# Attention's queue order: transposes ahead of near scores, output copies with the sum of the same step

## The chip, the cores and the metric

The kernel runs on one core of a Trainium2 chip. A core has engines that work side by side, each through its own queue in order: TensorE (matrix products and transposes, PE in the profile), VectorE (DVE), ScalarE (ACT), GpSimd (POOL) and SyncE (SP, which here only issues DMAs). The engines meet through semaphores. TensorE writes to PSUM, a small memory of eight banks; VectorE and ScalarE read results there. The metric is device time in microseconds for one execution.

## The reference

One decoder layer on 2048 tokens of width 1024, in float32: a mixer (attention beside pooling), a gated MLP, a gated embedding and a last norm. The change touches the attention alone: 8 heads of width 64, three dilated sliding windows, mixed by their softmax denominators.

```python
DIL_PATTERNS = ((128, 1), (512, 4), (2048, 16))

def _dilated_branch(q, k, v, slopes, window, dil):
    ...
    s = s - slopes[:, None, None] * dist
    s = jnp.where(valid[:, None, None], s, -jnp.inf)
    m = jnp.max(s, axis=-1, keepdims=True)
    e = jnp.exp(s - m)
    den = jnp.sum(e, axis=-1)
    o = jnp.einsum('bnrhqk,bnkrhd->bnqrhd', e, vv.astype(jnp.float32))
    ...

def _dilated_attention(q, k, v, slopes):
    ...
    w = d * jnp.exp(m - jnp.max(m, axis=0, keepdims=True))
    w = w / jnp.sum(w, axis=0, keepdims=True)
    return jnp.sum(w[..., None] * o, axis=0)
```

## The kernel before

The kernel runs in phases: projection, attention (399 to about 691 us of the profiled span), output product, MLP, gated embedding. Products are done on pairs of float32r tiles, a high part and a low part, to keep float32's precision.

Attention works through 128 steps, 16 blocks of 128 queries for each of 8 heads. In a step the "near" part is the window of stride 1 (up to 256 keys), the "far" part joins the two dilated windows (128 to 512 keys). Inside a group of four steps the blocks are taken in the order 3, 1, 2, 0, so the far part of steps 0, 1, 2 and 3 of a group has 512, 256, 384 and 128 keys. Two heads form a pair; even heads keep their output on partitions 0 to 63, odd heads on 64 to 127.

The order of every engine's queue is written out by hand. The loop at L744 goes through the steps, and for each step through `CFG["ord"]`, a list of pairs of a stage's name and a lag: stage X with lag d works in step s on the block of step s - d. The place in the list sets the order of the instructions in each engine's queue. The stages:

- N, F (`near_scores`, L574 and L575; `far_scores`, L563 and L564): two products each on TensorE, queries' high and low parts. The near scores of all steps share one PSUM bank, even steps in one half, odd steps in the other; far scores have two banks.
- nm, fm (`near_max`, L579; `far_max`, L585), VectorE: bias added, and the extreme of each row. The profile shows them as a custom operation with a short read of the accumulator behind it.
- ne, fe (`near_exp`, L591; `far_exp`, L595), ScalarE: exponentials with their row sums. A stage A allocates their tile.
- T (`turn`, L605), TensorE: 2 to 6 transposes of 128 x 128 into PSUM; two buffers alternate from step to step (tags t and u).
- h (`high`, L618), ScalarE, and l (`low`, L622), VectorE: high and low part of the transposed tile. The low part is the last reader of the transposes' bank.
- V and W (`values`, `values_b`, L633 and L647), TensorE: products with the values. They work on whole groups of four steps: parts 0 and 1 the far output, parts 2 and 3 the near output, into one PSUM tile each.
- o (`fold`, copy at L664), ScalarE: after parts 1 and 3, so in every other step, a copy of the other 64 partitions of the output. It puts the sum that belongs to it into the list `due`. p (`folded`, sum at L665), VectorE: takes everything that lies in `due` and adds.
- S, M (`stats`, `mix`): at the end of a head pair the maxima and denominators are transposed, copied and stored to DRAM, loaded again in another layout (ScalarE's DMAs), turned into weights (small operations on VectorE) and used by GpSimd to mix the outputs.
- B begins a step and issues nothing.

So before, step s holds in each queue, with the lag in brackets: TensorE V(7), W(7), N(0), T(2), F(0); VectorE fm(1), p, l(3), statistics, nm(0); ScalarE M's DMAs, o(7), ne(1), fe(1), h(2).

Of the kernel before, what the change touches and what calls it, by code (L numbers as in the profile page):

```python
# [10 lines left out]
F32 = mybir.dt.float32  # L11
# [6 lines left out]
P = 128  # L18
D = 1024
KD = D // P  # L20
S = 2048
# [5 lines left out]
CH = 512  # L27
# [13 lines left out]
V_N = V_CB + 2 * NF  # L41


CFG = {"tt": 2, "ee": 2, 'ord': [['B', 0], ['A', 1], ['M', 0], ['V', 7], ['fm', 1], ['W', 7], ['N', 0], ['p', 8], ['T', 2], ['F', 0], ['o', 7], ['ne', 1], ['fe', 1], ['h', 2], ['l', 3], ['S', 2], ['nm', 0]], 'perm': [3, 1, 2, 0], 'fp': [[0], [1], [2], [3]], 'np': [[0, -1], [1], [2], [3]], 'm': [9, 10, 13, 4, 6, 7]}


class Shared:
# [438 lines left out]
def phase_attention(tc, g, mx, near_b, far_b):  # L486
# [5 lines left out]
    with ExitStack() as ctx:  # L492
# [4 lines left out]
        ps_o = ctx.enter_context(tc.tile_pool(name="b_o", bufs=2, space=PSUM, reuse_waits="tile"))  # L497
# [37 lines left out]
        def begin(s):  # L535
# [7 lines left out]
            st = steps[s] = Shared()  # L543
            st.n = n = n - n % 4 + CFG["perm"][n % 4]
            st.t, st.pt, st.e = heads[h], pairs[h // 2], h % 2
# [5 lines left out]
            st.d1, st.d3 = st.pt.st1[:, 1, st.e, n : n + 1], st.pt.st3[:, st.r, 1, st.e, st.i : st.i + 1]  # L551
            st.tt = sb.tile([P, 768], F32, tag="tt", bufs=CFG["tt"], name="tt")

        def exp_tile(s):
            steps[s].ee = sb.tile([P, 768], F32, tag="ee", bufs=CFG["ee"], name="ee")

# [67 lines left out]
        def near_pv(gi, kbs, first):  # L624
            gr, q0 = groups[gi], 4 * (gi % 4)
            for kb in kbs:
                if q0 + kb < 0:
                    continue
                m0, m1 = max(0, kb), min(3, kb + 1)
                b0, b1 = 4 * m0 + kb + 1, 4 * m1 + kb + 1  # L630
                kt = q0 + kb
                for pt in (gr.h, gr.l):
                    nc.tensor.matmul(  # L633
                        gr.o[:, m0 * P : (m1 + 1) * P],
                        vals[gi // 8, "v1", kt // 4][:, kt % 4, gi // 4 % 2, :],
                        pt[:, b0 : b1 + 1 : 4, :],
                        start=first,
                        stop=False,
                        skip_group_check=True,
                    )  # L640
                    first = False

        def far_pv(gi, kbs, first):
            gr = groups[gi]
            for kb in kbs:
                for pt in (gr.h, gr.l):
                    nc.tensor.matmul(  # L647
                        gr.o[:, kb * P :],
                        vals[gi // 8, "v3", gi % 4][:, kb, gi // 4 % 2, :],
                        pt[:, 6 * kb + 2 : 18 + kb : 5, :],  # L650
                        start=first,
                        stop=False,
                        skip_group_check=True,
                    )
                    first = False
# [3 lines left out]
        def halves_sum(dst, o, e):  # L659

            mine = slice(DH * e, DH * e + DH)
            other = slice(DH * (1 - e), DH * (1 - e) + DH)
            ev = sb.tile([P, CH], F32, tag="ev", bufs=2, name="ev")
            nc.scalar.copy(ev[mine], o[other])  # L664
            due.append(lambda: nc.vector.tensor_tensor(dst, o[mine], ev[mine], op=ALU.add))  # L665

        def values(v):
            gi, part = v // 4, v % 4
            gr = groups[gi]
            if part % 2 == 0:  # L670
                gr.o = ps_o.tile([P, CH], F32, tag="o", name="o")
            if part < 2:
                far_pv(gi, CFG["fp"][2 * part], part == 0)
            else:
                near_pv(gi, CFG["np"][2 * part - 4], part == 2)

        def values_b(v):
            gi, part = v // 4, v % 4
            if part < 2:
                far_pv(gi, CFG["fp"][2 * part + 1], False)  # L680
            else:
                near_pv(gi, CFG["np"][2 * part - 3], False)

        def fold(v):
            gi, part = v // 4, v % 4
            if part % 2 == 0:
                return
            gr = groups[gi]
            h, q = divmod(gi, 4)
            pt, e = pairs[h // 2], h % 2  # L690
            mine = slice(DH * e, DH * e + DH)
            if part == 1:
                halves_sum(pt.s3[mine, q, :], gr.o, e)
            else:
                halves_sum(pt.s1[mine, q * CH : (q + 1) * CH], gr.o, e)
                groups.pop(gi)

        def folded(v):
# [34 lines left out]
        with tc.manual_schedule(engines=set(EN.values())):  # L733
            for dst, src in load_qk(0):
                rdma(nc, dst, src)
            for q in range(4):
                for which in ("v3", "v1"):
                    rdma(nc, *load_v(0, which, q))
            queue = []
            stages = {  # L740
                "F": far_scores, "N": near_scores, "fm": far_max, "nm": near_max, "fe": far_exp, "ne": near_exp,
                "T": turn, "h": high, "l": low, "V": values, "W": values_b, "S": stats, "M": mix, "o": fold, "p": folded, "B": begin, "A": exp_tile
            }
            for s in range(NS + 10):  # L744
                if s < NS:
                    h, n = divmod(s, NQ)
                    if n == 1 and h + 1 < H:
                        queue += load_qk(h + 1)
                    if queue:
                        rdma(nc, *queue.pop(0))  # L750
                    for pr in range(1, NPAIR):
                        if s - 2 * NQ * (pr - 1) in V_STEPS:
                            rdma(nc, *load_v(pr, *V_STEPS[s - 2 * NQ * (pr - 1)]))
                if s == NS + 2:
                    last_far(nc, g, mx, ps_t, pairs[NPAIR - 1])
                    pieces = pairs[NPAIR - 1].pieces = last_weights(nc, mx, pairs[NPAIR - 1])
                for nm, lag in CFG["ord"]:
                    if 0 <= s - lag < NS or nm == "M":
                        stages[nm](s - lag)
                for _ in range({NS + 3: 3, NS + 4: 2, NS + 5: 1}.get(s, 0)):  # L760
                    next(pieces)
# [1214 lines left out]
```

## Time and profile before

| | us |
|---|---|
| median of 3 runs | 2417.68 (2416.0 to 2421.61) |
| profiled execution | 2422.34 |
| its span, first to last instruction | 2420.6 |
| TensorE, VectorE, ScalarE, GpSimd busy in the span | 2329.2, 1711.4, 1140.5, 547.7 |

In a row of the timeline the columns are start (us from the span's start), duration (us), engine, line, operation, output and inputs with their shapes, count, and in brackets the idle time of the engine just before with what ended it. A row of the waits gives who waited, for whom, and the total in us, the number of times and the longest. Where an operation starts before the one ahead of it on its engine has ended, the two overlap in the engine's pipeline; the time from start to start is then what one operation costs.

### The profile page before, as it was taken

Reading aid. Unit: us, or ns where it says so; the run is one execution under the profiler, and the core shown is the slowest. Engines: PE = TensorE matmul, PEld = TensorE weight load, DVE = VectorE, ACT = ScalarE, POOL = GpSimd, SP = SyncE. Lnnn points to the kernel's source line nnn. Section 1 sums busy time; section 2 is a strip of 40 time slices with the busy share of each in tenths; the row PEclk is TensorE's granted clock in tenths of the full one; section 3 lists DMA queues with packets and bytes.
Section 4 is the critical chain, followed back from the end, with each engine's and each line's share of the span. In section 5 each row is a group of like instructions: output and inputs, shape, how many; then the busy total and the mean of one; then the engine's idle time right before and its main releaser. Section 6 shows DMA issues by size and latency. Waiting matters only on the chain.

```text
span 2420.6 us, 32492 instructions
## 1 busy us (share of the span) xinstructions
PE 2329.2 (96%) x11251; PEld 1963.2 (81%) x11251; DVE 1711.4 (71%) x2705; ACT 1140.5 (47%) x2055; POOL 547.7 (23%) x552
## 2 busy tenths in 40 slices
PE   8999999898879999999999999999999999999998
PEld 7888887888858878888888787788878888888888
DVE  6644445888872458999999998877766565755665
ACT  5433325888841135444446544444444444543332
POOL 3322221054520123334431566100020000001000
PEclk9999999999999999999999999999999999999999
DMA  7534437556556675455666787444488676654332
GB/s 233 179 138 174 163 137 268 215 198 191 186 196 232 215 251 169 167 200 191 212 203 228 267 274 263 163 151 142 136 308 271 226 253 208 218 168 158 122 100 92
DMA packets 248132, 476.05 MB, mean 197 GB/s; under 512 B 47361, under 2 KB 73793, under 8 KB 244897
## 3 DMA queue, kind: packets, MB, share of 16 engines
q1 hardware_dynamic: 198992, 385.20, 47.6%
q0 software_dynamic: 29328, 61.02, 7.3%
q10 hardware_dynamic: 19648, 27.77, 3.3%
q8 instruction: 88, 1.44, 0.3%
q14 instruction: 76, 0.61, 0.1%
HBM read 313.08 MB, written 160.73 MB: 196 GB/s over the span
## 4 chain that ended last, share of the span: by engine, by line
PE 75%; DVE 10%; DMA 4%; issue 4%; ACT 2%; POOL 0%; SPq 0%; ACTq 0%; DVEq 0%; POOLq 0%
PE ua L1324 17%; PE uc L1324 8%; PE dn L90 5%; PE dn L91 5%; PE dn L89 5%; PE ub L1324 4%; PE z L91 4%; PE z L89 4%; PE z L90 4%; PE gp L89 2%; PE gp L91 2%; PE gp L90 2%; PE o L89 2%; PE o L91 2%; PE o L90 2%
## 5 line engine op out<-in xcount | busy, mean ns | idle before, releaser
L90 PE MATMUL dn<-al,wu 128*128 128x512 f32 x616 | 240.2, 390 | 3.9 <-DVE al L85 3.8
L89 PE MATMUL dn<-ah,wu 128*128 128x512 f32 x616 | 240.0, 390 | 0.0
L91 PE MATMUL dn<-ah,wu 128*128 128x512 f32 x616 | 239.8, 389 | 0.0
L85 DVE TENSOR_TENSOR al<-ra,ah 128x512 fp32r<-128x512 f32 x154 | 105.9, 690 | 108.2 <-ACT ah L84 106.2
L89 PE MATMUL z<-hnh,wh 128*128 128x512 f32 (+1 forms) x480 | 170.3, 355 | 9.9 <-ACT hnh L252 6.2
L90 PE MATMUL z<-hnl,wh 128*128 128x512 f32 (+1 forms) x480 | 170.0, 354 | 3.1 <-DVE hnl L253 3.0
L91 PE MATMUL z<-hnh,wl 128*128 128x512 f32 (+1 forms) x480 | 169.8, 354 | 2.3 <-POOL wl L85 1.7
L84 ACT CAST ah<-ra 128x512 fp32r<-128x512 f32 x154 | 95.4, 622 | 140.7 <-PE dn L91 128.1
L90 PEld LDWEIGHTS dn<-al,wu 128*128 128x128 f32 x616 | 115.6, 188 | 29.7 <-DVE al L85 5.6
L89 PEld LDWEIGHTS dn<-ah,wu 128*128 128x128 f32 x616 | 115.6, 188 | 24.1
L91 PEld LDWEIGHTS dn<-ah,wu 128*128 128x128 f32 x616 | 115.6, 188 | 23.9
L85 DVE TENSOR_TENSOR wu<-ru,wu 128x1024 fp32r<-128x1024 f32 x88 | 133.0, 1511 | 2.4 <-ACT wu L84 2.4
L1324 PE MATMUL ua<-s4h,wu 128*128 128x512 f32 x352 | 117.0, 394 | 2.0 <-ACT uv L1572 2.0
L1324 PE MATMUL ub<-a12h,wu 128*128 128x512 f32 x352 | 116.8, 392 | 1.6 <-ACT a12h L1380 1.6
L1324 PE MATMUL ua<-s1h,wu 128*128 128x512 f32 x352 | 115.7, 390 | 2.0 <-ACT ug L1551 2.0
L1324 PE MATMUL ua<-s2h,wu 128*128 128x512 f32 x352 | 116.0, 391 | 1.0 <-ACT ug L1525 0.7
L1324 PE MATMUL uc<-a22h,wu 128*128 128x512 f32 x352 | 115.8, 390 | 0.6 <-DVE uv L1347 0.6
L85 DVE TENSOR_TENSOR wu<-rw,wu 128x512 fp32r<-128x512 f32 x149 | 101.0, 688 | 21.2 <-ACT wu L84 21.1
L1324 PE MATMUL uc<-s3h,wu 128*128 128x512 f32 x352 | 115.6, 389 | 0.0
L1324 PE MATMUL ua<-a11h,wu 128*128 128x512 f32 x352 | 115.5, 389 | 0.0
L155 DVE TENSOR_TENSOR acc<-acc,sq 128x512 f32<-128x512 f32 (+1 forms) x125 | 81.2, 649 | 43.9 <-ACT sq L154 30.2
L89 PEld LDWEIGHTS z<-hnh,wh 128*128 128x128 f32 x480 | 94.2, 196 | 22.0 <-ACT hnh L252 6.2
(336 smaller groups left out, 6644.4 us busy)
## 6 DMA issues: line engine op xcount, KB each, us to landing
ru<-in_w_up_dram SPq DMA_DIRECT2D x66, 512.0 KB, 4.2
wr<-in_w_in_dram SPq DMA_DIRECT2D x64, 256.0 KB, 4.3
rw<-in_w_down_dram SPq DMA_DIRECT2D x61, 256.0 KB, 3.7
nt<-h SPq DMA_DIRECT2D x56, 256.0 KB, 4.2
td<-t SPq DMA_DIRECT2D x22, 512.0 KB, 2.6
t<-td SPq DMA_DIRECT2D x22, 512.0 KB, 3.6
nt<-in_w_down_dram POOLq DMA_DIRECT2D x44, 256.0 KB, 5.4
ra<-oq0s SPq DMA_DIRECT2D x44, 256.0 KB, 4.1
```

What stands on the lines that cost most here:

```text
L84: nc.scalar.copy(hi, src)
L85: (low or nc.gpsimd).tensor_tensor(lo, src, fp(hi), op=ALU.subtract)
L89: nc.tensor.matmul(ps, wh, ah, start=first, stop=False, skip_group_check=again)
L90: nc.tensor.matmul(ps, wh, al, start=False, stop=False, skip_group_check=again)
L91: nc.tensor.matmul(ps, wl, ah, start=False, stop=last, skip_group_check=again)
L155: nc.vector.tensor_tensor(acc[:, :n], acc[:, :n], sq[:, :n], op=ALU.add)
L1324: nc.tensor.matmul(pst, x[:, ksl], y, start=first and k == 0 and n == 0, stop=k == HK - 1 and n == 2, skip_group_check=True)
```

## The change

The list of stages gets another order and other lags, and the output tile of a group becomes a list of two, since the far output is now copied after the near output's tile has been allocated.

```diff
-CFG = {"tt": 2, "ee": 2, 'ord': [['B', 0], ['A', 1], ['M', 0], ['V', 7], ['fm', 1], ['W', 7], ['N', 0], ['p', 8], ['T', 2], ['F', 0], ['o', 7], ['ne', 1], ['fe', 1], ['h', 2], ['l', 3], ['S', 2], ['nm', 0]], 'perm': [3, 1, 2, 0], ...
+CFG = {"tt": 2, "ee": 2, 'ord': [['B', 0], ['A', 1], ['M', 0], ['ne', 1], ['o', 8], ['fm', 1], ['fe', 1], ['p', 9], ['l', 3], ['V', 7], ['W', 7], ['T', 2], ['N', 0], ['nm', 0], ['h', 2], ['F', 0], ['S', 2]], 'perm': [3, 1, 2, 0], ...
...
-                        gr.o[:, m0 * P : (m1 + 1) * P],
+                        gr.o[1][:, m0 * P : (m1 + 1) * P],
...
-                        gr.o[:, kb * P :],
+                        gr.o[0][:, kb * P :],
...
             if part % 2 == 0:
-                gr.o = ps_o.tile([P, CH], F32, tag="o", name="o")
+                gr.__dict__.setdefault("o", []).append(ps_o.tile([P, CH], F32, tag="o", name="o"))
...
             if part == 1:
-                halves_sum(pt.s3[mine, q, :], gr.o, e)
+                halves_sum(pt.s3[mine, q, :], gr.o[0], e)
             else:
-                halves_sum(pt.s1[mine, q * CH : (q + 1) * CH], gr.o, e)
+                halves_sum(pt.s1[mine, q * CH : (q + 1) * CH], gr.o[1], e)
```

After it, step s holds: TensorE V(7), W(7), T(2), N(0), F(0); VectorE fm(1), p, l(3), nm(0), statistics; ScalarE M's DMAs, ne(1), o(8), fe(1), h(2). No instruction is added or taken away.

More of the change, by code (lines that the diff above doesn't have):

```diff
@@ L41 @@
 V_N = V_CB + 2 * NF
-CFG = {"tt": 2, "ee": 2, 'ord': [['B', 0], ['A', 1], ['M', 0], ['V', 7], ['fm', 1], ['W', 7], ['N', 0], ['p', 8], ['T', 2], ['F', 0], ['o', 7], ['ne', 1], ['fe', 1], ['h', 2], ['l', 3], ['S', 2], ['nm', 0]], 'perm': [3, 1, 2, 0], 'fp': [[0], [1], [2], [3]], 'np': [[0, -1], [1], [2], [3]], 'm': [9, 10, 13, 4, 6, 7]}
+CFG = {"tt": 2, "ee": 2, 'ord': [['B', 0], ['A', 1], ['M', 0], ['ne', 1], ['o', 8], ['fm', 1], ['fe', 1], ['p', 9], ['l', 3], ['V', 7], ['W', 7], ['T', 2], ['N', 0], ['nm', 0], ['h', 2], ['F', 0], ['S', 2]], 'perm': [3, 1, 2, 0], 'fp': [[0], [1], [2], [3]], 'np': [[0, -1], [1], [2], [3]], 'm': [9, 10, 13, 4, 6, 7]}
 class Shared:
```

## The prediction

> **What bounds the kernel now.** The change touches attention only, so I cut that stretch out first (windows, 399 to 690 us: width; TensorE matmul, weight load, VectorE, ScalarE, GpSimd busy; granted clock; DMA), then asked who waits in it (waits, one line an engine).
>
> ```profile
> span 2420.6 us, 32492 instructions
> 399.00:690.00 291.00, 257.67 (x1673) 240.06 (x1671) 238.77 (x743) 250.15 (x708) 109.66 (x116) 0.99 0.59 200
> PE sn L574 <- DVE st L579: 22.9, 48, 1.7
> DVE tt L585 <- PE sf L564: 36.4, 57, 1.2
> ACT ev L664 <- PE o L647: 6.6, 23, 0.3
> ```
>
> No engine is full: TensorE 89%, ScalarE 86%, VectorE 82%. TensorE waits for the near maximum (L579), VectorE for the far scores (L564), ScalarE for the output products (L647): a ring of short waits, so the order of each queue sets the time. The pace is read from the first near exponentials (L591) of steps 8, 32, 36, 64, 68, 96, 100 and 124, in the timeline:
>
> ```profile
> 416.50 0.51 ACT L591 ACTIVATE ee<-tt,st 128x256 f32<-128x256 f32 x1
> 466.26 0.51 ACT L591 ACTIVATE ee<-tt,st 128x256 f32<-128x256 f32 x1
> 478.79 0.51 ACT L591 ACTIVATE ee<-tt,st 128x256 f32<-128x256 f32 x1
> 537.01 0.51 ACT L591 ACTIVATE ee<-tt,st 128x256 f32<-128x256 f32 x1
> 550.81 0.51 ACT L591 ACTIVATE ee<-tt,st 128x256 f32<-128x256 f32 x1
> 609.83 0.51 ACT L591 ACTIVATE ee<-tt,st 128x256 f32<-128x256 f32 x1
> 623.41 0.51 ACT L591 ACTIVATE ee<-tt,st 128x256 f32<-128x256 f32 x1
> 672.87 0.51 ACT L591 ACTIVATE ee<-tt,st 128x256 f32<-128x256 f32 x1
> ```
>
> 49.76 + 58.22 + 59.02 + 49.46 = 216.5 us for 26 periods of four steps: 8.33 us a period. Between them lie three changes of head pair, 12.5 to 13.8 us each. One ring, in steps 75 to 77:
>
> ```profile
> 565.46 0.41 DVE L579 CUSTOM_DVE_ANT_0 tt<-sn,nb 128x256 f32<-128x256 f32 x1
> 565.93 0.39 PE L574 MATMUL sn<-ks,qhh 128*128 128x256 f32 x1 [0.21 <-DVE st L579]
> 566.27 0.71 PE L605 MATMUL tp<-ident,ee 128*128 128x128 f32 x5
> 566.74 0.60 PE L563 MATMUL sf<-ks,qhh 128*128 128x512 f32 x1
> 567.61 0.69 DVE L585 CUSTOM_DVE_ANT_0 tt<-sf,fb 128x512 f32<-128x512 f32 x1 [0.58 <-PE sf L564]
> 568.23 0.68 DVE L665 TENSOR_TENSOR s<-o,ev 64x512 f32<-64x512 f32 x1
> 568.83 0.81 DVE L622 TENSOR_TENSOR ptl<-tp,pth 128x640 fp32r<-128x640 f32 x1
> 569.56 0.41 DVE L579 CUSTOM_DVE_ANT_0 tt<-sn,nb 128x256 f32<-128x256 f32 x1
> ```
>
> Near maximum of step 75, near scores of 76, transposes of 74, far scores of 76, far maximum, sum of output halves, low parts, near maximum of 77: 4.10 us for two steps. The near scores wait for the maximum of the step before (both halves lie in one bank), and the transposes stand behind them.
>
> **The change part by part.** *TensorE*: transposes go ahead of the near scores. They need the low parts (L622) that free their bank, which end just before the near maximum, so they run under it and the near and far scores come about 0.33 us earlier in each even step (the transposes' own 0.47 us from start to the far scores, less the 0.14 us by which low parts free them after the maximum has begun: 568.83 + 0.81 against 569.56 gives 0.08, and about 0.06 for the signal). By itself that takes 0.66 us from the ring of a period.
>
> *VectorE*: its queue keeps far maximum, sum, low parts, near maximum; the list now names the near maximum ahead of the far scores, but the two are on different engines. Only at three head-pair ends does it pass the statistics' two copies. *GpSimd and SP*: mixing and loads keep their places, so no DMA is moved past anything on those queues; on ScalarE the three stores and loads of statistics stay at the head of their steps.
>
> *ScalarE*: near exponential, copy of the other output half, far exponential, high parts; before, the copy led. The decisive edit is in the lags. Before, step s made its copy (lag 7) after the sums of that step had been taken from the list, so a sum found a copy made a step earlier. Now the copy has lag 8 and stands ahead of the sums, which empty the whole list: the copy moves a step later, **the sum does not**, and it waits for a copy issued in its own step. Behind that waiting sum on VectorE stand the low parts and the near maximum; for these wait the transposes, the next near scores and the next near exponential. That closes a ring in each odd step: near exponential, copy, sum, low parts, near maximum, next near exponential. Its links, by rows:
>
> ```profile
> 567.95 0.52 ACT L591 ACTIVATE ee<-tt,st 128x256 f32<-128x256 f32 x1
> 568.46 0.72 ACT L595 ACTIVATE ee<-tt,st 128x512 f32<-128x512 f32 x1
> 548.85 0.58 ACT L664 COPY ev<-o 64x512 f32<-64x512 f32 x1 [3.36 <-PE sn L575]
> 549.46 0.69 DVE L665 TENSOR_TENSOR s<-o,ev 64x512 f32<-64x512 f32 x1 [1.46 <-ACT ev L664]
> 516.39 0.94 DVE L622 TENSOR_TENSOR ptl<-tp,pth 128x768 fp32r<-128x768 f32 x1
> 517.26 0.40 DVE L579 CUSTOM_DVE_ANT_0 tt<-sn,nb 128x256 f32<-128x256 f32 x1
> 401.36 0.40 DVE L579 CUSTOM_DVE_ANT_0 tt<-sn,nb 128x256 f32<-128x256 f32 x1
> 401.81 0.51 ACT L591 ACTIVATE ee<-tt,st 128x256 f32<-128x256 f32 x1 [1.69 <-DVE st L579]
> 528.88 0.69 DVE L665 TENSOR_TENSOR s<-o,ev 64x512 f32<-64x512 f32 x1
> 529.60 0.82 DVE L622 TENSOR_TENSOR ptl<-tp,pth 128x640 fp32r<-128x640 f32 x1
> ```
>
> Near exponential to the next ScalarE operation 0.51 (567.95 to 568.46); copy to its waiting sum 0.61 (548.85 to 549.46); sum to low parts 0.60 (568.23 to 568.83), but 0.72 where the sum belongs to an odd head and starts at partition 64 (528.88 to 529.60); low parts to near maximum 0.73 for 640 columns (568.83 to 569.56) and 0.87 for 768 (516.39 to 517.26); near maximum to its exponential 0.45 (401.36 to 401.81). So 2.90 us for steps 1 of 4 and 3.04 for steps 3 of 4, 0.12 more in odd heads. An even step has no copy; ScalarE sets it, at its quickest:
>
> ```profile
> 542.13 0.51 ACT L591 ACTIVATE ee<-tt,st 128x256 f32<-128x256 f32 x1
> 543.82 0.51 ACT L591 ACTIVATE ee<-tt,st 128x256 f32<-128x256 f32 x1
> 535.54 0.51 ACT L591 ACTIVATE ee<-tt,st 128x256 f32<-128x256 f32 x1
> ```
>
> 1.69 (542.13 to 543.82) and 1.47 (535.54 to 537.01). **Sum**: 2.90 + 1.69 + 3.04 + 1.47 = 9.10 us a period in even heads, 9.34 in odd. Of the 26 periods the sums of 16 are of even heads: 16 × 9.10 + 10 × 9.34 = 239.0, against 216.5: **+22.5 us**. The 0.33 us gained on TensorE is then hidden: the far maximum is ready about 1 us before the sum's copy.
>
> Two more terms. The weights' small operations delay the far maximum, and the far exponential behind it:
>
> ```profile
> 561.30 0.18 DVE L879 TENSOR_TENSOR dn<-wts,sn 128x32 f32<-128x32 f32 x1
> 562.37 0.42 DVE L585 CUSTOM_DVE_ANT_0 tt<-sf,fb 128x256 f32<-128x256 f32 x1
> 562.83 0.51 ACT L595 ACTIVATE ee<-tt,st 128x256 f32<-128x256 f32 x1 [0.76 <-DVE st L585]
> ```
>
> They take 1.07 us (561.30 to 562.37). My 216.5 us holds them, my 9.10 does not: 0.34 + 1.07 + 0.46 (562.37 to 562.83), less the 0.45 + 0.51 in which ScalarE gets there, is 0.9 us, and the step before, with the first exponentials of the weights, I estimate at 0.5 (three such operations beside five): 3 × 1.4 = **+4 us** (bounds 0 and 6). The head-pair changes I take at zero (bounds -3 and +2): statistics are stored and loaded again, and the load's issue waits for the store:
>
> ```profile
> 540.38 0.46 ACTq L781 DMA_DIRECT2D std<-sx  x1
> 547.75 0.45 ACTq L789 DMA_DIRECT2D sn<-std  x1
> ```
>
> Those 7.4 us cover the added waits of the steps between. Start (no copies in the first nine steps) and end cancel, within 1 us.
>
> Total 22.5 + 4 = +26.5, say **+27 us**. The profiled execution took 2422.34 us (its span and 1.7 around it), 4.7 above the median of 2417.68; it becomes 2449, and the median **2445**.
>
> One link can be priced by the Trainium skill. VectorE: DVE Perf Modes, section "The DRAIN you can't avoid", says that the next operation does not start until the pipeline has emptied; sum and low parts would then cost their full 0.68 and 0.81 or 0.94 (0.3 us a period more in even heads, 16 × 0.3 = 5 us, an estimate by that page). The same page's section "Two Vector instructions with no wait between them" lets an operation that starts in the same quadrant begin earlier; the 0.60 us beside 0.72 agrees with this one, so the sum above stands.
>
> **The rivals.** *Faster*: the sum finds its copy ready, as it would if it too came a step later. Then the gain on TensorE counts: the ring of a period goes from twice 4.10 to 8.20 - 0.66 = 7.54, and 7.78 in odd heads (0.12 for each of two sums): 16 × 7.54 + 10 × 7.78 = 198.4, or -18 us: 2400. It decides where the copy ends before the far maximum does. For it: VectorE now idles 0.58 us ahead of a far maximum. Against: a near exponential at 567.95 comes after the far maximum at 567.61, and the copy now stands behind it. Chance 0.08.
>
> *Same*: the first wait merely shifts ScalarE ahead of VectorE, the waits of L574 and L564 absorb it, and the old pace holds: 2418. Against it: the new ring goes through ScalarE itself and cannot be shifted away. Chance 0.05.
>
> *Much slower*: the longer waits lower the granted clock. It was 0.99 over attention, with single waits of TensorE up to 1.7 us. At half clock throughout, its 257.67 / 291 × 8.33 = 7.4 us a period would be 14.7, and 29 periods some 160 us longer: 2580; above a clock of 0.8 it costs nothing, since 7.4 / 0.8 fits into 9.2. Chance 0.05. (TensorE: Matmul & The Clock Gate in the Trainium skill, Part 1, has the clock halve after an idle window of about 3.4 us; the 1.7 us here fits with a clock that stayed up.)
>
> **How the numbers follow.** The ring through the copy 0.82, the rivals 0.08, 0.05 and 0.05. The forecast's own range: no mixing term and the low end of the head pairs, -7, and 5 for links that overlap better than in the rows: 2433; above, 2 for the mixing bound, 0.1 us of signalling on each of some 60 waiting sums and as much where high parts wait for transposes, 14 in all: 2459. To hold 8 in 10 I widen it to 2426 to 2462. A measurement of this kernel tells about 0.2%, 5 us, from no change: faster 0.08, same 0.05, slower 0.82 + 0.05 = 0.87.
>
> **What would show it.** Right: VectorE's sum (L665) waits about 1 us for ScalarE's copy (L664) in nearly all 64 cases, 4 before; ScalarE waits some 0.7 us for the near maximum ahead of the near exponential in odd steps; the waits of L574 and L564 shrink; a period takes 9.1 to 9.4 us. Wrong: if sums don't wait, or periods stay under 8.5 us, the ring is not there; if transposes still start after the near scores, the TensorE part failed.

## The result and the profile after

The changed kernel takes 2459.68 us (median of 4, 2456.89 to 2463.89), against 2419.64 us for the kernel before beside it (median of 4): 1.0168 of it, interval 1.0146 to 1.0191. Measured again in a second session it was 1.0132 (1.0117 to 1.0147; 2453.97 against 2420.62). The forecast was 2445, slower by 27; it is slower by 33 to 40, near the upper end of the range 2426 to 2462.

The page's first line and the waits of the changed kernel, 399 to 725 us (who waited, for whom: us in total, times, longest):

```profile
span 2455.1 us, 32493 instructions
```

```profile
DVE s L665 <- ACT ev L664: 57.4, 62, 3.3
DVE tt L579 <- PE sn L575: 6.3, 15, 1.2
...
DVE tt L585 <- PE sf L564: 0.8, 4, 0.3
...
ACT ee L591 <- DVE st L579: 43.3, 55, 1.7
...
PE tp L605 <- DVE ptl L622: 57.8, 55, 1.9
...
PE sn L574 <- DVE st L579: 1.7, 1, 1.7
```

The waits of before are gone: VectorE's for the far scores fell from 36.4 to 0.8 us, and TensorE's for the near maximum from 22.9 us in 48 cases to a single one. In their place VectorE's sum waits for ScalarE's copy in 62 cases of 64, ScalarE's near exponential for the near maximum, and TensorE's transposes for the low parts. That is the chain copy, sum, low parts, near maximum, exponential, each waiting for the one before. Odd step 77 of the timeline shows it, both engines together:

```profile
586.50 0.51 ACT L591 ACTIVATE ee<-tt,st 128x256 f32<-128x256 f32 x1
...
587.12 0.58 ACT L664 COPY ev<-o 64x512 f32<-64x512 f32 x1
...
587.61 0.72 ACT L595 ACTIVATE ee<-tt,st 128x512 f32<-128x512 f32 x1
...
587.74 0.68 DVE L665 TENSOR_TENSOR s<-o,ev 64x512 f32<-64x512 f32 x1 [0.71 <-ACT ev L664]
...
588.35 0.81 DVE L622 TENSOR_TENSOR ptl<-tp,pth 128x640 fp32r<-128x640 f32 x1
...
589.08 0.41 DVE L579 CUSTOM_DVE_ANT_0 tt<-sn,nb 128x256 f32<-128x256 f32 x1
...
589.59 0.51 ACT L591 ACTIVATE ee<-tt,st 128x256 f32<-128x256 f32 x1 [0.66 <-DVE st L579]
```

From exponential to exponential 3.09 us, link by link 0.62, 0.62, 0.61, 0.73, 0.51. The forecast had 0.51, 0.61, 0.60, 0.73, 0.45 = 2.90. The near exponentials that begin the same four stretches as before (steps 8, 32, 36, 64, 68, 96, 100, 124):

```profile
416.12 0.51 ACT L591 ACTIVATE ee<-tt,st 128x256 f32<-128x256 f32 x1
...
473.40 0.51 ACT L591 ACTIVATE ee<-tt,st 128x256 f32<-128x256 f32 x1
...
485.53 0.51 ACT L591 ACTIVATE ee<-tt,st 128x256 f32<-128x256 f32 x1
...
553.38 0.51 ACT L591 ACTIVATE ee<-tt,st 128x256 f32<-128x256 f32 x1
...
566.10 0.51 ACT L591 ACTIVATE ee<-tt,st 128x256 f32<-128x256 f32 x1
...
634.04 0.51 ACT L591 ACTIVATE ee<-tt,st 128x256 f32<-128x256 f32 x1
...
646.35 0.51 ACT L591 ACTIVATE ee<-tt,st 128x256 f32<-128x256 f32 x1
...
704.77 0.51 ACT L591 ACTIVATE ee<-tt,st 128x256 f32<-128x256 f32 x1
```

57.28 + 67.85 + 67.94 + 58.42 = 251.5 us for the 26 regular periods, 216.5 before: +35.0, as much as the whole span grew (2455.1 - 2420.6 = 34.5). The three changes of head pair between them give back 2.75 us (12.13 + 12.72 + 12.31 against 39.91), and the end of attention, from the last near exponential to the first cast of the output product's weights, takes 2.15 us more (712.98 to 727.36 us against 680.15 to 692.38). Of these, 1.32 us lie ahead of the statistics' transposes (L819), where one more sum waits 1.47 us for its copy. The other 0.83 us are those eight transposes themselves: 1.86 us, at a granted clock of 0.50, against 1.03 us at 1.00 before. Around them the clock is 0.67 (windows, 720 to 730 us, same columns as in the prediction):

```profile
720.00:730.00 10.00, 7.31 (x30) 5.81 (x27) 6.88 (x9) 4.97 (x8) 0.00 (x0) 0.67 0.33 105
```

### The profile page after: what moved, and what is told of

Read it like the earlier page. It is cut to its first block, busy times and chain, and to the rows that moved or that the text cites. A ratio compares the mean times of both kernels' runs of the same rounds, so it can differ in the third digit from the quotient of the medians.

```text
span 2455.1 us, 32493 instructions
## 1 busy us (share of the span) xinstructions
PE 2327.9 (95%) x11251; PEld 1963.7 (80%) x11251; DVE 1718.6 (70%) x2705; ACT 1141.8 (47%) x2055; POOL 547.0 (22%) x552
## 4 chain that ended last, share of the span: by engine, by line
PE 68%; DVE 10%; ACT 7%; issue 6%; DMA 5%; POOL 0%; SPq 0%; ACTq 0%; DVEq 0%; POOLq 0%
PE ua L1324 15%; PE uc L1324 8%; PE dn L90 5%; PE dn L91 5%; PE dn L89 5%; PE ub L1324 4%; PE z L89 4%; PE z L91 4%; PE z L90 4%; ACT ee L591 3%; PE gp L89 2%; PE gp L90 2%; PE gp L91 2%; PE o L91 2%; PE o L89 2%
## 5 line engine op out<-in xcount | busy, mean ns | idle before, releaser
L605 PE MATMUL tp<-ident,ee 128*128 128x128 f32 x568 | 86.7, 280 | 61.0 <-DVE ptl L622 57.8
L605 PEld LDWEIGHTS tp<-ident,ee 128*128 128x128 f32 x568 | 65.2, 143 | 69.6 <-ACT pth L618 64.0
```

Of the source, the lines that this page charges most:

```text
L605: nc.tensor.transpose(st.tp[:, bs], st.ee[:, bs], g.ident)
```

## The experiments

Each alters the order list, or a line or two, of the changed kernel; runs 2 and 8 start from the kernel before. The ratio is to the kernel before in the same session; "26 periods" is the sum formed as above, from the profiled execution of each run (before 216.5, changed 251.5).

The changed kernel ran again beside runs 5 to 7:

> The changed kernel once more, unaltered, as the measure for the three runs beside it on the same chip. All theories: 1.014 to 1.019 of the time before.

| run | ratio (95%) | 26 periods, us |
|---|---|---|
| changed, again | 1.0132 (1.0117 to 1.0147) | 251.5 |
| 1 sum a step later | 0.9918 (0.9903 to 0.9932) | 205.9 |
| 1 again | 0.9939 (0.9926 to 0.9951) | 207.3 |
| 2 before, transposes first | 0.9949 (0.9927 to 0.9971) | 206.3 |
| 3 near scores first again | 1.0162 (1.0142 to 1.0182) | 260.7 |
| 4 copy ahead of near exponential | 1.0025 (1.001 to 1.004) | 227.2 |
| 5 copy of all partitions | 1.0108 (1.0083 to 1.0132) | 245.7 |
| 6 sum later and near scores first | 0.9922 (0.9898 to 0.9945) | 205.6 |
| 7 copy behind far exponential | 1.0343 (1.032 to 1.0367) | 293.6 |
| 8 before, sum in even steps | 0.9941 (0.9927 to 0.9955) | 206.9 |

**1, the sum a step later.**

```diff
-['ne', 1], ['o', 8], ['fm', 1], ['fe', 1], ['p', 9], ['l', 3],
+['ne', 1], ['fm', 1], ['p', 9], ['o', 8], ['fe', 1], ['l', 3],
```

> The changed kernel, with the taking of the sums from the list put ahead of the step's copy, so that a sum finds a copy made one step earlier; ScalarE's and TensorE's queues stay as changed. Ring theory: the ring exponential, copy, sum, low parts, near maximum is opened, VectorE's sums (L665) wait under 6 us in all, and ScalarE's work (about 7.8 us a period of four steps: two odd steps of 2.30, even ones of 1.69 and 1.47) sets the pace: 26 regular periods near 203 us, some 14 us less than before the change, time 2400 to 2410 us. Rival (the loss is in the new order itself, the copies' and exponentials' place or the transposes', not in the sum's wait): stays above 2445 us.

2407.35 us against 2426.07 before in that session: 0.9918. The rival, that the new order itself costs, falls: the other queue orders are as changed, and 45 us of the 251 are gone. The first lines of VectorE's waits hold no sum any more (399 to 725 us):

```profile
DVE ptl L622 <- ACT pth L618: 10.1, 13, 3.1
DVE lwo L85 <- DMA xc<-in_xT_dram: 6.5, 1, 6.5
DVE tt L579 <- PE sn L575: 3.1, 6, 0.9
```

A regular period is now 7.7 to 7.8 us (odd steps 2.2 to 2.3, even ones 1.68 and 1.47). ScalarE is busy 7.60 of the 7.70 us of the one from step 52, and its near exponentials wait for the near maximum only 7 times, 2.7 us in all: the bound has moved to ScalarE. Note that this edit also moves the sum from an odd step to an even one; run 8 comes back to that.

**2, transposes ahead of near scores, all else as before.**

```diff
-['W', 7], ['N', 0], ['p', 8], ['T', 2], ['F', 0],
+['W', 7], ['T', 2], ['N', 0], ['p', 8], ['F', 0],
```

> The kernel before, with only the transposes put ahead of the near scores on TensorE. Ring theory: the ring through near scores and far scores loses 0.66 us a period, ScalarE becomes the bound near 7.8 to 7.9 us a period, and the time falls by 9 to 13 us, to 2405 to 2410 us; the waits of L574 for the near maximum nearly vanish. Rival (ScalarE paced it already, the waits on TensorE and VectorE were slack): within 4 us of before. Rival (transposes first are what costs): slower than before.

26 periods lose 10.2 us, the time falls to 0.9949, and TensorE waits for the near maximum (L574) once, 1.7 us, where it was 48 times and 22.9. So this part of the change alone is a gain, and both rivals fall.

**3, near scores back ahead of the transposes in the changed kernel.**

```diff
-['W', 7], ['T', 2], ['N', 0], ['nm', 0],
+['W', 7], ['N', 0], ['T', 2], ['nm', 0],
```

> The changed kernel with the near scores put back ahead of the transposes. Ring theory: the transposes are not on the ring through the copy; it stays at 2456 to 2466 us (a little above the changed kernel if the high parts of even steps now wait for their transposes, up to 0.2 us a step). Rival (transposes first are what costs): falls to about 2420 us.

Not faster: 26 periods grow by 9.2 us more. The whole time doesn't tell it from the changed kernel (1.0162 beside 1.0168 and 1.0132). Two views answer for it, VectorE's and ScalarE's waits (399 to 725 us):

```profile
DVE s L665 <- ACT ev L664: 44.9, 60, 1.7
DVE tt L585 <- PE sf L564: 38.4, 57, 1.5
...
ACT pth L618 <- PE tp L605: 4.9, 14, 0.8
```

The far scores are late again (38.4 us, 36.4 before), but these waits lie beside the sum's; what costs is behind the last row. In even steps the high parts come late with the transposes, and such a step takes 1.86 and 1.64 us where it took 1.68 and 1.47, 0.35 us a period or 9.1 in 26. The row shows only part of it, since ScalarE counts as busy while the short read behind the far exponential runs. From that read to the high parts, in the changed kernel and then in this run:

```profile
614.00 0.18 ACT L595 ACTIVATION_READ_ACCUMULATOR ee<-tt,st 128x1 f32 x1
614.10 0.67 ACT L618 CAST pth<-tp 128x640 fp32r<-128x640 f32 x1
```

```profile
621.44 0.19 ACT L595 ACTIVATION_READ_ACCUMULATOR ee<-tt,st 128x1 f32 x1
621.69 0.69 ACT L618 CAST pth<-tp 128x640 fp32r<-128x640 f32 x1
```

**4, the copy ahead of the near exponential, in the step of its sum.**

```diff
-['M', 0], ['ne', 1], ['o', 8], ['fm', 1],
+['M', 0], ['o', 8], ['ne', 1], ['fm', 1],
```

> The changed kernel with the copy put back ahead of the near exponential on ScalarE, still with lag 8 and in the step of its sum. Ring theory: the near exponential of the odd step leaves the ring; copy to sum 0.62, sum to low parts 0.61, low parts to near maximum 0.73 or 0.86, to the exponential 0.51, then the even step's 1.69 or 1.47: 8.23 us a period, 8.47 in odd heads, about the pace before the change: 2412 to 2422 us, with the sums still waiting for the copies. Rival (a sum in the step of its copy costs wherever the copy stands): 2450 us or more.

1.0025, between theory and rival but near the theory: undisturbed periods take 8.42 to 8.55 us in even heads (8.19 with the narrower near part of a head's first block) and 8.65 in odd ones, where 8.23 and 8.47 were worked out. With the copy ahead of the exponential, 24 us of the 35 come back; the place of the copy decides, not the mere fact that it shares a step with its sum. The 26 periods stay 11 us above before (227.2 against 216.5). About 7 of these lie in the six periods with mixing (9.30 against 8.54 for the one from step 40) and the rest in the undisturbed ones, 0.2 to 0.3 us each above the links' sum. What makes either longer, no run settles.

**5, the copy without moving partitions.**

```diff
-            nc.scalar.copy(ev[mine], o[other])
+            nc.scalar.copy(ev, o)
```

> The changed kernel, with the copy made of all 128 partitions from partition 0 to partition 0 in place of 64 partitions moved to the other half; the sum then adds an output half to itself, not to the other half. Same columns, same waits, same order. In the changed kernel the copy starts 0.62 us after the near exponential, once that has wholly ended, where the far exponential started 0.51 us after it. Theory (the copy is held because its input or output starts at another partition): 0.51 again, 0.11 us less in each odd step, 26 periods shorter by about 5.7 us, time 5 to 8 us below the changed kernel's; behind the copy the far exponential starts after 0.49 us in odd heads too, 0.60 before. Rival (it is held for its wait on a semaphore, or because its input lies in PSUM): 0.62 stays, same time.

ScalarE's timeline in that run:

```profile
579.38 0.51 ACT L591 ACTIVATE ee<-tt,st 128x256 f32<-128x256 f32 x1
...
579.88 0.57 ACT L664 COPY ev<-o 128x512 f32<-128x512 f32 x1
...
580.35 0.62 ACT L595 ACTIVATE ee<-tt,st 128x384 f32<-128x384 f32 x1
```

The copy starts 0.50 us after the near exponential, and 60 of the 64 do so after 0.50 or 0.51, where it was 0.62 or 0.63; the far exponential follows after 0.46 to 0.47 us in all heads, where it was 0.49 in even and 0.60 in odd ones. 26 periods are 5.8 us shorter, as expected, and the median 8 us. The copy's wait on a semaphore and its input in PSUM are the same in both, so they don't hold it. The run changes two things, though: where the copy starts, and 128 partitions in place of 64. The changed kernel's own trace tells these apart. All its copies have 64 partitions; even heads' read from partition 64 and write to 0, odd heads' read from 0 and write to 64. Only behind the odd heads' is the next operation held (0.60 against 0.49). And only in even heads is the next operation that reads PSUM held, the high parts (L618) behind the far exponential: they start 0.21 or 0.22 us after the accumulator read ahead of them began in all 32 such steps, mostly 0.09 or 0.10 in odd heads and in run 5. An even head's step, an odd head's, and run 5:

```profile
588.24 0.19 ACT L595 ACTIVATION_READ_ACCUMULATOR ee<-tt,st 128x1 f32 x1
588.45 0.48 ACT L618 CAST pth<-tp 128x384 fp32r<-128x384 f32 x1
...
616.53 0.19 ACT L595 ACTIVATION_READ_ACCUMULATOR ee<-tt,st 128x1 f32 x1
616.62 0.46 ACT L618 CAST pth<-tp 128x384 fp32r<-128x384 f32 x1
```

```profile
580.87 0.20 ACT L595 ACTIVATION_READ_ACCUMULATOR ee<-tt,st 128x1 f32 x1
580.96 0.57 ACT L618 CAST pth<-tp 128x512 fp32r<-128x512 f32 x1
```

So these later holds follow the start partition, not the number of partitions. The hold ahead of the copy is alike in both kinds of head; that it has the same cause is inferred.

**6, sum later and near scores first.**

```diff
-['ne', 1], ['o', 8], ['fm', 1], ['fe', 1], ['p', 9], ['l', 3], ['V', 7], ['W', 7], ['T', 2], ['N', 0],
+['ne', 1], ['fm', 1], ['p', 9], ['o', 8], ['fe', 1], ['l', 3], ['V', 7], ['W', 7], ['N', 0], ['T', 2],
```

> The changed kernel with the sum a step after its copy (as in the first experiment) and the near scores back ahead of the transposes. Ring theory: with the copy's ring open, the ring of near maximum, near scores, transposes, far scores, far maximum is the longest again, about 8.25 us a period, more in odd heads: 26 periods 213 to 218 us, time within 5 us of before. Rival (ScalarE's work sets the pace as soon as the sum doesn't wait, whatever TensorE's order): 26 periods near 206 us, some 18 us below before.

This one went against my theory, which said 213 to 218: TensorE's and VectorE's queues have the order of before (but for the statistics at three head-pair ends), and yet 26 periods take 205.6 us, as the rival said. What had I left out? A sum a step later stands in an even step. Run 8 was made to tell that from the copy's new place.

**7, the copy behind the far exponential.**

```diff
-['ne', 1], ['o', 8], ['fm', 1], ['fe', 1], ['p', 9],
+['ne', 1], ['fm', 1], ['fe', 1], ['o', 8], ['p', 9],
```

> The changed kernel with the copy put behind the far exponential on ScalarE, in the same step, so that the far exponential too lies on the ring. Ring theory: an odd step becomes 0.51 + 0.83 (or 0.73 for 384 columns) + 0.61 + 0.61 + 0.73 (or 0.86) + 0.51 = 3.80 or 3.83 us, even ones stay 1.68 and 1.47: 10.8 us a period in even heads, 11.0 in odd, against 9.46 and 9.68; 26 periods 35 us longer than the changed kernel's 251, time some 38 us above it, 1.030 to 1.034 of before. Rival (the sum's wait is taken up by slack beyond what was lost already): within 10 us of the changed kernel.

The ring grows as reckoned: undisturbed periods take 10.84 us in even heads and 11.07 in odd ones, 10.8 and 11.0 expected. But others reach 11.8, the 26 together grow by 42 us, not 35, and the time lies 49.5 us above the changed kernel's, not 38. Windows (399 to 760 us) and a stretch of TensorE's and VectorE's timeline show why:

```profile
399.00:760.00 361.00, 270.08 (x1623) 253.25 (x1622) 241.13 (x730) 253.96 (x699) 110.09 (x117) 0.90 0.46 161
```

```profile
542.65 0.56 PE L574 MATMUL sn<-ks,qhh 128*128 128x256 f32 x1
...
543.65 0.63 PE L564 MATMUL sf<-ks,qll 128*128 128x512 f32 x1
...
544.31 0.69 DVE L585 CUSTOM_DVE_ANT_0 tt<-sf,fb 128x512 f32<-128x512 f32 x1 [0.42 <-PE sf L564]
```

The granted clock fell to 0.90, with TensorE busy 270 of 361 us (75%). In the stretch shown it is 0.50 (542 to 545 us), the far scores' product takes 0.63 us instead of 0.39, and VectorE waits for it. Apart from the first period and those with mixing, all periods at a clock of 0.96 or more are undisturbed (10.63 to 10.85 us, 11.07 in odd heads); of the twelve at 0.95 or less, ten are longer, by 5.6 us together, most of the 7 missing.

**8, the sum a step later, all queues as before.**

```diff
-            due.append(lambda: nc.vector.tensor_tensor(dst, o[mine], ev[mine], op=ALU.add))
+            due.append((v, lambda: nc.vector.tensor_tensor(dst, o[mine], ev[mine], op=ALU.add)))
...
-            while due:
-                due.pop(0)()
+            while due and due[0][0] <= v:
+                due.pop(0)[1]()
```

(`halves_sum` gets v from `fold`, and p the lag 9.)

> The kernel before, all queues in its order, but a sum is taken only when its copy is two steps old, so that the sums move from odd steps to even ones. Theory (new): in odd steps VectorE's sum lay on the ring between a far maximum of 512 or 384 columns and low parts of 768 or 640; in even steps it fits into the time in which VectorE waits for the far scores anyway, so the ring near scores, transposes, far scores loses 1.2 us a period, falls to about 7.05, and ScalarE's 7.8 us bound: 26 periods 203 to 208 us, against 216.5, and the time 10 to 14 us below before (ratio 0.993 to 0.996). Rival (the first kernel and the seventh gained from the copy's new place behind the near exponential, where it no longer waits for TensorE): no gain, within 4 us of before.

(The rival's first and seventh kernel are runs 1 and 6 here.)

206.9 and 0.9941, within both expected ranges, with the copy where it was before. The sum now stands behind the far maximum of 256 columns:

```profile
510.26 0.42 DVE L585 CUSTOM_DVE_ANT_0 tt<-sf,fb 128x256 f32<-128x256 f32 x1
...
510.61 0.68 DVE L665 TENSOR_TENSOR s<-o,ev 64x512 f32<-64x512 f32 x1
...
511.21 0.40 DVE L622 TENSOR_TENSOR ptl<-tp,pth 128x256 fp32r<-128x256 f32 x1
```

and the far maximum's waits for TensorE are few (399 to 690 us; 57 times and 36.4 us before):

```profile
DVE tt L585 <- PE sf L564: 6.2, 11, 1.3
```

Runs 1, 6 and 8 end at the same pace, 206 to 207 us for 26 periods, and so does run 2, which leaves the sums where they were and moves only the transposes. Run 1 again, beside run 8 in one session:

> The kernel of the first experiment once more, unaltered, on the same chip as the run beside it: all theories 0.990 to 0.994 of the time before.

It gave 0.9939, level with run 8. Each is 0.6% faster than the kernel before.

## Why the prediction came out as it did

**The sum waits for its copy: right.** The ring through ScalarE and VectorE is there in every odd step (62 waits of the sum), the waits of L574 and L564 shrank, and runs 1, 4 and 7, which open it, shorten it or lengthen it, move the time down, down and up. Run 7's undisturbed periods match the sum of their links within 0.1 us; run 4's stand 0.2 to 0.3 us above it. Of the signs named, the sum's wait (57.4 / 62 = 0.93 us), ScalarE's wait for the near maximum (43.3 / 55 = 0.79 us) and the shrunk waits came as said. The period did not: 9.46 us in even heads (four shorter ones of 9.24 apart) and 9.68 in odd ones, above 9.1 to 9.4.

**Its size: the term "22.5 us" was too small by 8.5.** Measured is 35.0 for the regular periods, mixing included, against 22.5 + 4. Two links were read where the situation differed. Near exponential to copy takes 0.62 us, not 0.51: the row I used shows an exponential behind an exponential, and a copy that moves between partition halves starts only when the operation ahead has ended (run 5). Near maximum to exponential takes 0.51, not 0.45. The row of 0.45 is the very first step of attention, which takes 0.44 or 0.45 in every run, where waiting exponentials of 256 columns in later odd steps take 0.51 or so in every run that has them; why, no run settles. Together 0.17 us in each of 52 odd steps, 8.8 us. The range held because it allowed 0.1 us of signalling on each waiting sum and as much where high parts wait; that the cost lay in other links makes this in part luck.

**Mixing +4: right**, by its terms too: the step with the weights' small operations is 0.87 us longer than its neighbours, 0.9 said, the one with the first exponentials 0.31 to 0.49, 0.5 said; in all 3.9 us. **Head pairs at zero: wrong within its bound**, they gave back 2.75, near the -3. **Start and end cancel within 1 us: just missed.** From the first near exponential to that of step 8 the changed kernel takes 13.68 us, 1.01 less than before, but the end costs 2.15 more: +1.1. The end has a last turn of the ring in it, and a slow stretch of the clock that I did not expect.

**"The 0.33 us gained on TensorE is then hidden": wrong.** It holds for the far maximum, but I followed only that. The transposes also release the high parts in even steps, and these lie on the ring through ScalarE; run 3's 26 periods show that the changed kernel would be 9 us slower still without them first.

**The faster rival: nearly its price, on another ground.** I gave 2400, 18 us less, for a sum that finds its copy; run 1 is 13 to 19 us below the kernel before. Its 26 periods lose only 9 to 11 us, though, where the rival counted 18; another 4.5 to 5 come from the changes of head pair (39.91 us before, 34.89 and 35.38 in run 1), which it did not count. But I had kept the sum on the ring of scores and counted on the transposes' place. Run 6 shows that place to be worth nothing then, and run 8 that moving the sum into even steps is enough: there it fills time in which VectorE waited. ScalarE bounds next, at 7.7 to 7.8 us a period, and the 7.54 and 7.78 of the rival left that out in even heads.

**Clock: the rival did not decide here** (0.97 from 399 to 725 us), but it shows in run 7, whose undisturbed periods keep TensorE busy for 7.67 of 10.84 us (7.66 of 9.46 in the changed kernel, where the clock drops only near changes of head pair and at the end). Its stated floor, no cost above a clock of 0.8, was too easy: run 7's mean of 0.90 has stretches at 0.50 in it, and those already cost. Its price was miscounted too: 160 us is 29 times 14.7 less 9.2, so it stands above the forecast 2445, not above 2418, and gives about 2605, not 2580.

## What to carry to other kernels

When an order is written out by hand, look for what a wait closes into a ring: the price is the sum of the links from start to start, and here it was paid in every turn, though no engine was full. Ask also in which step the moved work lands: the same sums beside the longest operations lay on the ring (8.33 us a period), and in steps where VectorE waited anyway they did not (7.7 to 7.8, another engine's work). Take each link's duration from a row with the same neighbour in the queue, not merely the same operation.

## What the runs showed of the hardware

A ScalarE copy that reads or writes from partition 64 starts only after the operation ahead has ended (0.62 us behind a near exponential, 0.50 when it has all 128 and starts at partition 0 on both sides), and after a copy written to partition 64 the next operation waits likewise (0.60 against 0.49). After a copy that reads PSUM from partition 64, the next operation that reads PSUM, from partition 0, is held too, though the far exponential stands between, which doesn't read PSUM (it starts 0.21 us after the accumulator read ahead of it began, against 0.09). The Trainium skill, VectorE: DVE Perf Modes, section "Two Vector instructions with no wait between them", states such a hold for VectorE. These runs show the same pattern on ScalarE.

The granted clock dropped over a stretch whose TensorE was still busy 75% of the time (0.90 in run 7, with 3 us at 0.50), and to 0.67 in the ten microseconds at the end of attention, where TensorE was busy for 7.3 of 10. No single idle stretch of TensorE in run 7's regular steps (404 to 660 us) was longer than 2.2 us. No run changes the idle time alone, so what the clock answers to stays open.
